# Attention logits: each head on its own 64 rows of the array, without zero-padded queries

## The chip, the cores and the metric

The kernel runs on one core of one Trainium2 chip. The metric is device time in microseconds (us) of one execution. Three runs of the kernel before took 1189.86, 1189.64 and 1187.67 us; the median is 1189.64.

## What is computed

A trunk of four layers on a sequence of 256 tokens of width 1024, all in fp32. Layers 0 and 3 are stick-breaking attention, layer 1 a short convolution, layer 2 gated linear attention; each is followed by a squared-ReLU MLP. Only the attention layers are changed. They have 16 heads of 64 dimensions:

```
z = jnp.einsum('bhqd,bhkd->bhqk', qb, k) * scale
mask = key_pos[None, :] < q_pos[:, None]
log_beta = jax.nn.log_sigmoid(z)
log_1m_beta = jnp.where(mask, jax.nn.log_sigmoid(-z), 0.0)
suffix = lax.cumsum(log_1m_beta, axis=3, reverse=True) - log_1m_beta
weights = jnp.where(mask, jnp.exp(log_beta + suffix), 0.0)
return jnp.einsum('bhqk,bhkd->bhqd', weights, v)
```

## The kernel before

Precision first, since it sets the count of matmuls. TensorE's one-pass fp32 type (fp32r) rounds its operands, so every operand that matters is split into a high part (rounded by ACT) and a low part (the rest, by DVE), and a product is three matmuls: high x high, high x low, low x high. Plain fp32 operands are taken as well; each such product appears as two passes in the trace. All matmuls go through the helper `mm` (line 113), so they share one line and are told apart by tile names: `acc` and `wk` are PSUM tiles (1024 columns in two banks, 512 in one), `hi` and `lo` split weights, `xt` the split input, `cr` and `onesr` constants, `s` anything in the pool of 20 slots of SBUF.

Weights come in by DMA (`raw`, line 207), ACT makes `hi` (line 220) and DVE makes `lo` (line 230). A list fixed in advance gives their order, and a counter how far ahead of use they are made ready.

An attention layer (`sb`, line 558) first makes v for all heads (in layer 0 this belongs to a hand-ordered opening, line 957), then goes over 4 groups of 4 heads, that is of 2 pairs. Two heads of 64 dimensions share the 128 partitions of a q or k tile.

- `qk_steps` (line 575) makes a group's q and k with the weights as the loaded operand: 48 products of 256 columns for each, then the splits. q's is done in two ACT and two DVE instructions of 64 rows each (lines 584 and 586), because each head's queries go to a place of their own: `qpad` has, for each pair of heads, 2 x 256 columns in which head 0 fills rows 0 to 63 of the first 256 and head 1 rows 64 to 127 of the second, and the rest is zero. `padded` (line 552) zeroes four such tiles per layer, on POOL in layer 0 and on DVE in layer 3. k's split is one instruction on each engine (lines 256 and 257).
- `logits` (line 596) handles a pair of heads at a time. Keys are loaded on all 128 rows, and a padded query column meets only its own head's rows. Keys 0 to 127 against all queries of both heads give 512 columns (one bank of the tile `z`), keys 128 to 255 against the later half of the queries 256 columns of the second bank. Two products with the identity put the causal mask (-1e30) in first. Then ACT and DVE make softplus(z) from Abs, Exp and Ln (lines 610 to 615), split in high and low (lines 617 and 618).
- `suffix` (line 621) adds the cumulative sums onto z by products with a triangular matrix of -1 and with a matrix of -1 (`onesr`): per part (high, low) three products of 256, 512 and 256 columns. ACT then takes Exp (line 632).
- `mixed` (line 636) multiplies the weights with v in plain fp32. A head's 64 output dimensions are 64 columns of the array, so these products use the left or the right half of the columns (`128*64` in the trace); they go into the last 256 columns of the second bank, one head on partitions 0 to 63, the other on 64 to 127.

PE's order in the loop over groups (from line 652) is the written one: for each group `logits`, then a stretch of the next group's q and k products (or of the output projection, in the last group) that covers the ACT and DVE chain, then `suffix`, another stretch, and `mixed` for both pairs. `FG` and `FO` (line 67) say how long the stretches are; a step of them is counted at 0.65 us, so 7.15 means 11 steps of six products. The other engines' order is that of a scheduler with priorities.

Of the kernel before, what the change touches and what calls it, by code (L numbers as in the profile page):

```python
# [20 lines left out]
SEQ = 256  # L21
# [41 lines left out]
def hybrid_kernel(ctx: ExitStack, tc: tile.TileContext, x, norm_gains, sb_w_qkv, sb_w_o,  # L63
# [5 lines left out]
    nc = tc.nc  # L69
# [24 lines left out]
    def T(pl, shape, dt, tag):  # L94
        return pl.tile(shape, dt, tag=tag, name=nm(tag))
# [16 lines left out]
    def mm(o, l, r, start, stop):  # L112
        nc.tensor.matmul(out=o, lhsT=l, rhs=r, start=start, stop=stop, skip_group_check=True)  # L113
# [4 lines left out]
    h = []  # L118
# [34 lines left out]
    for kind, l in phases:  # L153
# [14 lines left out]
        elif kind == "sb":  # L168
            w = sb_w_qkv[l // 3]
# [5 lines left out]
        elif kind == "conv":  # L175
            w = conv_w_in[0]
# [5 lines left out]
        else:  # L182
            w = gla_w_in[0]
# [71 lines left out]
    def split(hi, lo, src):  # L255
        nc.scalar.copy(out=hi, in_=src)  # L256
        nc.vector.tensor_tensor(out=lo, in0=src, in1=hi.bitcast(F32), op=ALU.subtract)  # L257
# [187 lines left out]
    def u_pair():  # L445
        return slot((P, 4, SEQ), F32R), slot((P, 4, SEQ), F32R)
# [102 lines left out]
            finish(parts[t] if final and t == NT - 1 else [accs[t]], t)  # L549


    def padded(eng, qpad):
        for i in range(4):
            q = slot((P, 2, 2, SEQ), F32R)
            eng.memset(q.bitcast(F32), 0.0)
            qpad.append(q)

    def sb(l, finish):
        qpad = early[0] if l == 0 else []
        vs = []  # L560
        if l == 0:
            accs = early[1]
        for t in range(NT):
            acc = accs[t] if l == 0 else x_proj(t, (l, "v"))
            v = slot()
            if t == 0:
                nc.vector.tensor_copy(out=v, in_=acc)
            else:
                nc.scalar.copy(out=v, in_=acc)
            vs.append(v)  # L570
            if l and t == 0:
                padded(nc.vector, qpad)
        us = [u_pair(), u_pair()]

        def qk_steps(g, res):
            w = wk_tile()
            yield from w_stat_steps(w, (l, "q", g))

            qh, ql = qpad[2 * (g % 2):2 * (g % 2) + 2]
            wv = w.rearrange("p (a b) -> p a b", b=SEQ)  # L580
            rows_of = [slice(0, 64), slice(64, 128)]
            with tc.high_priority(offset=EP):
                for hd, rs in enumerate(rows_of):
                    nc.scalar.activation(out=qh[rs, :, hd, :], in_=wv[rs, :, :], func=AF.Copy, scale=0.125)
                for hd, rs in enumerate(rows_of):
                    nc.vector.scalar_tensor_tensor(out=ql[rs, :, hd, :], in0=wv[rs, :, :], scalar=0.125,
                                                   in1=qh[rs, :, hd, :].bitcast(F32), op0=ALU.mult, op1=ALU.subtract)
            qs = [(qh[:, j, :, :], ql[:, j, :, :]) for j in range(2)]
            w = wk_tile()
            yield from w_stat_steps(w, (l, "k", g))  # L590
            k = slot((P, 2, 512), F32R)
            with tc.high_priority(offset=EP):
                split(k[:, 0, :], k[:, 1, :], w)
            res[g] = (qs, k)

        def logits(pairs):
            res = []
            for q, k in pairs:
                z = acc_tile()
                z0, z1 = z[:, 0:512], z[:, 512:768]  # L600
                z0v = z0.rearrange("p (a b) -> p a b", b=SEQ)
                mm(z0v[:, :, 0:P], ident_r, msk_r.rearrange("p (a b) -> p a b", b=P), True, False)
                mm(z1, ident_r, msk_r, True, False)
                for a, b in ((0, 0), (0, 1), (1, 0)):
                    mm(z0, k[:, a, 0:P], q[b].rearrange("p a b -> p (a b)"), False, False)
                for a, b in ((0, 0), (0, 1), (1, 0)):
                    mm(z1, k[:, a, P:2 * P], q[b][:, :, P:2 * P], False, False)
                res.append((z, scratch()[:, 0:768], scratch()[:, 0:768], slot((P, 768), F32R), slot((P, 768), F32R)))
            for z, a, sp, sh, sl in res:
                nc.scalar.activation(out=a, in_=z[:, 0:768], func=AF.Abs)  # L610
            for z, a, sp, sh, sl in res:
                nc.scalar.activation(out=a, in_=a, func=AF.Exp, scale=-1.0)
            for z, a, sp, sh, sl in res:
                nc.scalar.activation(out=a, in_=a, func=AF.Ln, bias=1.0)
                nc.vector.scalar_tensor_tensor(out=sp, in0=z[:, 0:768], scalar=0.0, in1=a, op0=ALU.max, op1=ALU.add)
            for z, a, sp, sh, sl in res:
                nc.scalar.copy(out=sh, in_=sp)
                nc.vector.tensor_tensor(out=sl, in0=sp, in1=sh.bitcast(F32), op=ALU.subtract)
            return [(z, sh, sl) for z, a, sp, sh, sl in res]

        def suffix(zs):
            wts = []
            for z, sh, sl in zs:
                z0, z1 = z[:, 0:512], z[:, 512:768]
                z0v = z0.rearrange("p (a b) -> p a b", b=SEQ)
                for n, s in enumerate((sh, sl)):
                    s1 = s[:, 512:768]
                    mm(z1, tri_r, s1, False, n == 1)
                    mm(z0, tri_r, s[:, 0:512], False, False)
                    mm(z0v[:, :, P:2 * P], ones_r, s1.rearrange("p (a b) -> p a b", b=P), False, n == 1)  # L630
                wt = scratch()[:, 0:768]
                nc.scalar.activation(out=wt, in_=z[:, 0:768], func=AF.Exp)
                wts.append((z, wt))
            return wts

        def mixed(pr, zw):
            z, wt = zw
            o = z[:, 768:1024]
            for hd in range(2):
                rows_ = slice(64 * hd, 64 * hd + 64)  # L640
                vc = slice(pr * P + 64 * hd, pr * P + 64 * hd + 64)
                mm(o[rows_, 0:SEQ], vs[0][:, vc], wt[:, hd * SEQ:(hd + 1) * SEQ], True, False)
                mm(o[rows_, P:SEQ], vs[1][:, vc], wt[:, 512 + hd * P:512 + (hd + 1) * P], False, True)
            split(us[pr // 4][0][:, pr % 4, :], us[pr // 4][1][:, pr % 4, :], o)

        rest_of_constants()
        qkv = {}
        Fill(qk_steps(0, qkv))()
        proj = out_proj_steps(l, us, finish)


        with tc.manual_schedule(engines={mybir.EngineType.PE}):
            for g in range(4):
                qs, k = qkv[g]
                fill = Fill(qk_steps(g + 1, qkv)) if g < 3 else Fill(proj)
                if l == 0:
                    ahead[0] = RAMP[g + 1]
                lead, before, after = FG[min(g, 1)] if g < 3 else FO
                fill(lead)
                with tc.high_priority(offset=AP):  # L660
                    zs = logits([(qs[0], k[:, :, 0:SEQ]), (qs[1], k[:, :, SEQ:512])])
# [285 lines left out]
    k, l = phases[0]  # L947
# [9 lines left out]
    def opening():  # L957
# [2 lines left out]

        g8 = slot((P, P))[0:KT, :]
        nc.scalar.dma_start(out=g8, in_=norm_gains[l, pre.get(k, 0), :].rearrange("(k p) -> k p", p=P))
        qpad = []
        padded(nc.gpsimd, qpad)
        still = slot((P, 512), F32R)
        jk = slot()
        accs = [acc_tile() for _ in range(NT)]
# [64 lines left out]
        with tc.manual_schedule(engines={mybir.EngineType.DVE, mybir.EngineType.Activation, mybir.EngineType.PE,  # L1032
# [63 lines left out]
        return qpad, accs  # L1096

    early = opening()
    outv = out.rearrange("b (t p) d -> (b t) p d", p=P)
# [42 lines left out]
```

## Time and profile before

| | us |
|---|---|
| median of three runs | 1189.64 |
| lowest and highest | 1187.67, 1189.86 |
| the profiled execution | 1188.06 |
| its span, from the first to the last instruction | 1186.3 |
| TensorE busy with matmuls (PE) | 1172.3 |
| TensorE busy with weight loads (PEld) | 1009.1 |
| VectorE (DVE) | 802.6 |
| ScalarE (ACT) | 675.1 |
| GpSimd (POOL) | 41.7 |

The mean granted TensorE clock is 0.999 of full speed. A row of the timeline has the start, the time to the end of the last instruction merged into the row, the engine, the line, the operation, the tiles (out<-in), for matmuls the rows x columns of the array that are used (128*128), the shape, and the count. Ends of matmuls are modelled and overlap the next matmul, so the pace is read from starts. Every matmul has a weight load of its own, on the row PEld.

### The profile page before, as it was taken

The numbers are of one execution on the slowest core, as the hardware profiler recorded it, in microseconds if no ns is written. First come the engines' busy times: TensorE is split into PE (matmuls) and PEld (weight loads), VectorE is DVE, ScalarE is ACT, GpSimd is POOL, SyncE is SP. The second block draws the span as 40 slices with busy tenths as digits, with TensorE's granted clock in tenths as the row PEclk, the third lists the DMA queues.
The fourth block names the chain that finished last, engine by engine and source line by source line (L and its number), as shares of the span: only waits on it lengthen the run. The fifth ranks groups of instructions, "written<-read, shape, count | busy, mean of one in ns | idle before, by whom it ended". The sixth has DMA issues, their size and how long they took to land.

```text
span 1186.3 us, 17257 instructions
## 1 busy us (share of the span) xinstructions
PE 1172.3 (99%) x6455; PEld 1009.1 (85%) x6455; DVE 802.6 (68%) x1280; ACT 675.1 (57%) x1212; POOL 41.7 (4%) x80
## 2 busy tenths in 40 slices
PE   8999999999999999999999999999999999999997
PEld 6998888888888888888889888888888998888886
DVE  6865876654878785765776778666658756855651
ACT  5886665543665564554573756545545875654540
POOL 1000100000100100000100010000000001000000
PEclk9999999999999999999999999999999999999999
DMA  7843576666576476666572356666647443666640
GB/s 243 280 125 107 165 244 190 186 196 193 161 234 207 144 236 194 192 193 216 151 242 87 111 161 223 193 197 184 212 145 230 138 157 111 217 195 192 191 146 36
DMA packets 126184, 214.24 MB, mean 181 GB/s; under 512 B 10954, under 2 KB 89042, under 8 KB 126100
## 3 DMA queue, kind: packets, MB, share of 16 engines
q1 hardware_dynamic: 125620, 212.54, 57.8%
q8 instruction: 50, 0.82, 0.3%
q10 hardware_dynamic: 448, 0.59, 0.1%
q14 instruction: 34, 0.28, 0.1%
q0 software_dynamic: 32, 0.00, 0.0%
HBM read 212.07 MB, written 1.05 MB: 180 GB/s over the span
## 4 chain that ended last, share of the span: by engine, by line
PE 93%; DVE 2%; issue 2%; ACT 1%; DMA 1%; POOL 0%; DVEq 0%; POOLq 0%; ACTq 0%
PE acc L113 69%; PE wk L113 22%; PE wk L297 2%; DVE lo L230 1%; DMA raw<-in_gla_w_in_dram 0%; DMA raw<-in_sb_w_qkv_dram 0%; ACT hi L220 0%; DVE lo L227 0%; ACT xt L999 0%; POOL sm L266 0%; DVE s L257 0%; ACT s L271 0%; ACT s L893 0%; DVE s L899 0%; ACT hi L222 0%
## 5 line engine op out<-in xcount | busy, mean ns | idle before, releaser
L230 DVE TENSOR_TENSOR lo<-raw,hi 128x512 fp32r<-128x512 f32 x752 | 492.1, 686 | 212.3 <-ACT hi L220 209.3
L220 ACT CAST hi<-raw 128x512 fp32r<-128x512 f32 x752 | 439.6, 620 | 317.8 <-PE acc L113 170.5
L113 PE MATMUL acc<-hi,s 128*128 128x512 f32 x1216 | 339.5, 391 | 0.0
L113 PEld LDWEIGHTS acc<-hi,s 128*128 128x128 f32 x1216 | 225.6, 188 | 45.8 <-ACT s L256 0.3
L113 PE MATMUL wk<-xt,hi 128*128 128x256 f32 (+1 forms) x1120 | 248.6, 309 | 0.0
L113 PE MATMUL wk<-xt,lo 128*128 128x256 f32 x704 | 196.9, 280 | 0.0
L113 PEld LDWEIGHTS wk<-xt,hi 128*128 128x128 f32 x1120 | 181.4, 188 | 12.8
L113 PE MATMUL acc<-lo,s 128*128 128x512 f32 x608 | 190.4, 390 | 0.0
L113 PE MATMUL acc<-xt,hi 128*128 128x512 f32 x512 | 179.6, 393 | 0.0
L113 PE MATMUL acc<-hi,xt 128*128 128x512 f32 x576 | 160.1, 394 | 0.8 <-ACT hi L220 0.8
L113 PE MATMUL acc<-xt,lo 128*128 128x256 f32 x512 | 143.2, 280 | 0.0
L113 PEld LDWEIGHTS acc<-lo,s 128*128 128x128 f32 x608 | 114.1, 188 | 23.8
L113 PEld LDWEIGHTS wk<-xt,lo 128*128 128x128 f32 x704 | 132.3, 188 | 0.0
L113 PEld LDWEIGHTS acc<-hi,xt 128*128 128x128 f32 x576 | 106.2, 188 | 24.5 <-ACT hi L220 2.3
L113 PEld LDWEIGHTS acc<-xt,hi 128*128 128x128 f32 x512 | 96.1, 188 | 21.0
L113 PEld LDWEIGHTS acc<-xt,lo 128*128 128x128 f32 x512 | 96.3, 188 | 0.9
L113 PE MATMUL acc<-lo,xt 128*128 128x512 f32 x288 | 88.9, 392 | 0.0
L113 PEld LDWEIGHTS acc<-lo,xt 128*128 128x128 f32 x288 | 53.8, 188 | 11.5 <-DVE lo L230 0.3
L284 DVE TENSOR_TENSOR s<-acc,s 128x1024 f32<-128x1024 f32 (+1 forms) x16 | 19.1, 1191 | 59.3 <-ACT s L271 59.0
L263 POOL TENSOR_SCALAR sm<-sm 128x1 f32<-128x1 f32 (+1 forms) x31 | 13.1, 423 | 1052.2 <-ACT s L271 992.8
L113 PE MATMUL acc<-s,s 128*128 128x256 f32 (+3 forms) x314 | 48.3, 330 | 1.0 <-DVE s L257 0.8
L271 ACT ACTIVATE s<-acc 128x1024 f32<-128x1024 f32 (+1 forms) x16 | 16.0, 998 | 57.1 <-PE acc L113 57.1
(125 smaller groups left out, 874.1 us busy)
## 6 DMA issues: line engine op xcount, KB each, us to landing
raw<-in_ffn_w_up_dram SPq DMA_DIRECT2D x128, 512.0 KB, 4.0
raw<-in_ffn_w_down_dram SPq DMA_DIRECT2D x128, 512.0 KB, 3.6
raw<-in_sb_w_qkv_dram SPq DMA_DIRECT2D x48, 512.0 KB, 5.1
raw<-in_conv_w_in_dram SPq DMA_DIRECT2D x24, 512.0 KB, 4.7
raw<-in_gla_w_in_dram SPq DMA_DIRECT2D x24, 512.0 KB, 3.8
raw<-in_sb_w_o_dram SPq DMA_DIRECT2D x16, 512.0 KB, 3.9
s<-in_norm_gains_dram SPq DMA_DIRECT2D x15, 512.0 KB, 5.2
raw<-in_conv_w_out_dram SPq DMA_DIRECT2D x8, 512.0 KB, 4.2
```

Of the source, the lines that this page charges most:

```text
L113: nc.tensor.matmul(out=o, lhsT=l, rhs=r, start=start, stop=stop, skip_group_check=True)
L220: nc.scalar.copy(out=hi[:, cs], in_=raw[:, cs])
L230: nc.vector.tensor_tensor(out=lo[:, cs], in0=raw[:, cs], in1=hi[:, cs].bitcast(F32), op=ALU.subtract)
L263: nc.gpsimd.tensor_scalar(out=v, in0=ss, scalar1=EPS, scalar2=None, op0=ALU.add)
L271: nc.scalar.activation(out=scratch()[:, 0:src.shape[1]], in_=src, func=AF.Square, scale=1.0 / 32.0, accum_out=ss)
L284: nc.vector.tensor_tensor(out=ag[:, cs], in0=a, in1=g[:, cs], op=ALU.mult)
L297: nc.tensor.transpose(out=dst[:, j * P:(j + 1) * P], in_=src[:, j * P:(j + 1) * P], identity=ident)
```

## The change

- `padded` and its calls go, and with them the zero-padded queries. q is split like k, by one ACT and one DVE instruction of 128 x 512, into a tile of its own for each group.
- `logits` now takes both pairs of a group. It puts in the masks of both pairs, then the q-k products. Each product uses one head's 64 rows of q and k (64*128): rows 0 to 63 for head 0, rows 64 to 127 for head 1, in turn. Each head has its own bank of z, in this order of columns: keys 128 to 255 with the later queries (128 columns), keys 0 to 127 with all queries (256), and the v product's output (128).
- `suffix` has per part two products of 384 columns with the triangular matrix, one per head, and two of 128 columns with the matrix of -1.
- `mixed` has three products of 128 columns per head, the two heads in turn; each half of the queries has its output in a bank.
- The tiles of the softplus chain have the shape 2 x 384 instead of 768, with the same number of elements.

The order of PE in the loop over groups, its stretches and the rest of the kernel stay as they are.

```diff
-    def padded(eng, qpad):
-        for i in range(4):
-            q = slot((P, 2, 2, SEQ), F32R)
-            eng.memset(q.bitcast(F32), 0.0)
-            qpad.append(q)
...
-            if l and t == 0:
-                padded(nc.vector, qpad)
...
+            q = slot((P, 2, 512), F32R)
             with tc.high_priority(offset=EP):
-                for hd, rs in enumerate(rows_of):
-                    nc.scalar.activation(out=qh[rs, :, hd, :], in_=wv[rs, :, :], func=AF.Copy, scale=0.125)
-                for hd, rs in enumerate(rows_of):
-                    nc.vector.scalar_tensor_tensor(out=ql[rs, :, hd, :], in0=wv[rs, :, :], scalar=0.125,
-                                                   in1=qh[rs, :, hd, :].bitcast(F32), op0=ALU.mult, op1=ALU.subtract)
-            qs = [(qh[:, j, :, :], ql[:, j, :, :]) for j in range(2)]
+                nc.scalar.activation(out=q[:, 0, :], in_=w, func=AF.Copy, scale=0.125)
+                nc.vector.scalar_tensor_tensor(out=q[:, 1, :], in0=w, scalar=0.125, in1=q[:, 0, :].bitcast(F32),
+                                               op0=ALU.mult, op1=ALU.subtract)
...
-            for q, k in pairs:
-                z = acc_tile()
-                z0, z1 = z[:, 0:512], z[:, 512:768]
-                z0v = z0.rearrange("p (a b) -> p a b", b=SEQ)
-                mm(z0v[:, :, 0:P], ident_r, msk_r.rearrange("p (a b) -> p a b", b=P), True, False)
-                mm(z1, ident_r, msk_r, True, False)
-                for a, b in ((0, 0), (0, 1), (1, 0)):
-                    mm(z0, k[:, a, 0:P], q[b].rearrange("p a b -> p (a b)"), False, False)
-                for a, b in ((0, 0), (0, 1), (1, 0)):
-                    mm(z1, k[:, a, P:2 * P], q[b][:, :, P:2 * P], False, False)
...
+            for j in range(2):
+                z = acc_tile().rearrange("p (h c) -> p h c", h=2)
+                for hd in range(2):
+                    mm(z[:, hd, 0:2 * P], ident_r, msk_r, True, False)
+                res.append((z, logit_tile(F32), logit_tile(F32), logit_tile(F32R), logit_tile(F32R)))
+            for j, (z, *_) in enumerate(res):
+                for ks, out in ((0, z[:, :, P:3 * P]), (P, z[:, :, 0:P])):
+                    for a, b in ((0, 0), (0, 1), (1, 0)):
+                        for hd in range(2):
+                            rs = slice(64 * hd, 64 * hd + 64)
+                            mm(out[:, hd, :], k[rs, a, j * SEQ + ks:j * SEQ + ks + P], q[rs, b, j * SEQ + ks:(j + 1) * SEQ],
+                               False, False)
...
                 for n, s in enumerate((sh, sl)):
-                    s1 = s[:, 512:768]
-                    mm(z1, tri_r, s1, False, n == 1)
-                    mm(z0, tri_r, s[:, 0:512], False, False)
-                    mm(z0v[:, :, P:2 * P], ones_r, s1.rearrange("p (a b) -> p a b", b=P), False, n == 1)
...
+                    for hd in range(2):
+                        mm(z[:, hd, 0:3 * P], tri_r, s[:, hd, :], False, False)
+                    for hd in range(2):
+                        mm(z[:, hd, 2 * P:3 * P], ones_r, s[:, hd, 0:P], False, n == 1)
...
-                mm(o[rows_, 0:SEQ], vs[0][:, vc], wt[:, hd * SEQ:(hd + 1) * SEQ], True, False)
-                mm(o[rows_, P:SEQ], vs[1][:, vc], wt[:, 512 + hd * P:512 + (hd + 1) * P], False, True)
...
+            for first, vt, ws, last_ in ((0, 0, 1, True), (1, 0, 2, False), (1, 1, 0, True)):
+                for hd in range(2):
+                    rs = slice(64 * hd, 64 * hd + 64)
+                    vc = slice(pr * P + 64 * hd, pr * P + 64 * hd + 64)
+                    mm(z[rs, first, 3 * P:4 * P], vs[vt][:, vc], wt[:, hd, ws * P:(ws + 1) * P], vt == 0, last_)
...
-        qpad = []
-        padded(nc.gpsimd, qpad)
```

More of the change, by code (lines that the diff above doesn't have):

```diff
@@ L549, in ffn @@
             finish(parts[t] if final and t == NT - 1 else [accs[t]], t)
-    def padded(eng, qpad):
-        for i in range(4):
-            q = slot((P, 2, 2, SEQ), F32R)
-            eng.memset(q.bitcast(F32), 0.0)
-            qpad.append(q)
     def sb(l, finish):
-        qpad = early[0] if l == 0 else []
         vs = []
         if l == 0:
-            accs = early[1]
+            accs = early
         for t in range(NT):
@@ L577, in qk_steps @@
             yield from w_stat_steps(w, (l, "q", g))
-            qh, ql = qpad[2 * (g % 2):2 * (g % 2) + 2]
-            wv = w.rearrange("p (a b) -> p a b", b=SEQ)
-            rows_of = [slice(0, 64), slice(64, 128)]
+            q = slot((P, 2, 512), F32R)
             with tc.high_priority(offset=EP):
-                for hd, rs in enumerate(rows_of):
-                    nc.scalar.activation(out=qh[rs, :, hd, :], in_=wv[rs, :, :], func=AF.Copy, scale=0.125)
-                for hd, rs in enumerate(rows_of):
-                    nc.vector.scalar_tensor_tensor(out=ql[rs, :, hd, :], in0=wv[rs, :, :], scalar=0.125,
-                                                   in1=qh[rs, :, hd, :].bitcast(F32), op0=ALU.mult, op1=ALU.subtract)
-            qs = [(qh[:, j, :, :], ql[:, j, :, :]) for j in range(2)]
+                nc.scalar.activation(out=q[:, 0, :], in_=w, func=AF.Copy, scale=0.125)
+                nc.vector.scalar_tensor_tensor(out=q[:, 1, :], in0=w, scalar=0.125, in1=q[:, 0, :].bitcast(F32),
+                                               op0=ALU.mult, op1=ALU.subtract)
             w = wk_tile()
@@ L593, in qk_steps, with logit_tile, logits @@
                 split(k[:, 0, :], k[:, 1, :], w)
-            res[g] = (qs, k)
-        def logits(pairs):
+            res[g] = (q, k)
+        def logit_tile(dt):
+            return slot((P, 2, 3 * P), dt)
+        def logits(q, k):
             res = []
-            for q, k in pairs:
-                z = acc_tile()
-                z0, z1 = z[:, 0:512], z[:, 512:768]
-                z0v = z0.rearrange("p (a b) -> p a b", b=SEQ)
-                mm(z0v[:, :, 0:P], ident_r, msk_r.rearrange("p (a b) -> p a b", b=P), True, False)
-                mm(z1, ident_r, msk_r, True, False)
-                for a, b in ((0, 0), (0, 1), (1, 0)):
-                    mm(z0, k[:, a, 0:P], q[b].rearrange("p a b -> p (a b)"), False, False)
-                for a, b in ((0, 0), (0, 1), (1, 0)):
-                    mm(z1, k[:, a, P:2 * P], q[b][:, :, P:2 * P], False, False)
-                res.append((z, scratch()[:, 0:768], scratch()[:, 0:768], slot((P, 768), F32R), slot((P, 768), F32R)))
+            for j in range(2):
[10 more added lines that the diff above has]
+                               False, False)
             for z, a, sp, sh, sl in res:
-                nc.scalar.activation(out=a, in_=z[:, 0:768], func=AF.Abs)
+                nc.scalar.activation(out=a, in_=z[:, :, 0:3 * P], func=AF.Abs)
             for z, a, sp, sh, sl in res:
@@ L614, in logits @@
                 nc.scalar.activation(out=a, in_=a, func=AF.Ln, bias=1.0)
-                nc.vector.scalar_tensor_tensor(out=sp, in0=z[:, 0:768], scalar=0.0, in1=a, op0=ALU.max, op1=ALU.add)
+                nc.vector.scalar_tensor_tensor(out=sp, in0=z[:, :, 0:3 * P], scalar=0.0, in1=a, op0=ALU.max, op1=ALU.add)
             for z, a, sp, sh, sl in res:
@@ L623, in suffix @@
             for z, sh, sl in zs:
-                z0, z1 = z[:, 0:512], z[:, 512:768]
-                z0v = z0.rearrange("p (a b) -> p a b", b=SEQ)
                 for n, s in enumerate((sh, sl)):
-                    s1 = s[:, 512:768]
-                    mm(z1, tri_r, s1, False, n == 1)
-                    mm(z0, tri_r, s[:, 0:512], False, False)
-                    mm(z0v[:, :, P:2 * P], ones_r, s1.rearrange("p (a b) -> p a b", b=P), False, n == 1)
-                wt = scratch()[:, 0:768]
-                nc.scalar.activation(out=wt, in_=z[:, 0:768], func=AF.Exp)
+                    for hd in range(2):
+                        mm(z[:, hd, 0:3 * P], tri_r, s[:, hd, :], False, False)
+                    for hd in range(2):
+                        mm(z[:, hd, 2 * P:3 * P], ones_r, s[:, hd, 0:P], False, n == 1)
+                wt = logit_tile(F32)
+                nc.scalar.activation(out=wt, in_=z[:, :, 0:3 * P], func=AF.Exp)
                 wts.append((z, wt))
@@ L637, in mixed @@
             z, wt = zw
[L638 to L641, printed above, removed]
-                mm(o[rows_, 0:SEQ], vs[0][:, vc], wt[:, hd * SEQ:(hd + 1) * SEQ], True, False)
-                mm(o[rows_, P:SEQ], vs[1][:, vc], wt[:, 512 + hd * P:512 + (hd + 1) * P], False, True)
-            split(us[pr // 4][0][:, pr % 4, :], us[pr // 4][1][:, pr % 4, :], o)
+            for first, vt, ws, last_ in ((0, 0, 1, True), (1, 0, 2, False), (1, 1, 0, True)):
[3 more added lines that the diff above has]
+                    mm(z[rs, first, 3 * P:4 * P], vs[vt][:, vc], wt[:, hd, ws * P:(ws + 1) * P], vt == 0, last_)
+            split(*(us[pr // 4][i][:, pr % 4, :].rearrange("p (h c) -> p h c", h=2) for i in range(2)),
+                  z[:, :, 3 * P:4 * P])
         rest_of_constants()
@@ L653, in sb @@
             for g in range(4):
-                qs, k = qkv[g]
+                q, k = qkv[g]
                 fill = Fill(qk_steps(g + 1, qkv)) if g < 3 else Fill(proj)
@@ L660, in sb @@
                 with tc.high_priority(offset=AP):
-                    zs = logits([(qs[0], k[:, :, 0:SEQ]), (qs[1], k[:, :, SEQ:512])])
+                    zs = logits(q, k)
                 fill(before)
@@ L1095, in opening @@
                         products(which, t, j)
-        return qpad, accs
+        return accs
     early = opening()
```

## The prediction

> **What bounds the kernel now.** I read the page first, then the chain of waits, then the attention layers in windows, then one head group instruction by instruction.
>
> ```profile
> span 1186.3 us, 17257 instructions
> PE 1172.3 (99%) x6455; PEld 1009.1 (85%) x6455; DVE 802.6 (68%) x1280; ACT 675.1 (57%) x1212; POOL 41.7 (4%) x80
> PE 93%; DVE 2%; issue 2%; ACT 1%; DMA 1%; POOL 0%; DVEq 0%; POOLq 0%; ACTq 0%
> ```
>
> TensorE is the chain. The windows of three head groups of the last layer say the same of the place that is changed (us, then PE, PEld, DVE, ACT, POOL busy, clock, DMA share):
>
> ```profile
> 922.90:938.90 16.00, 16.00 (x130) 15.05 (x130) 11.46 (x17) 13.97 (x24) 0.00 (x0) 1.00 0.37 127
> 938.90:956.40 17.50, 17.50 (x143) 16.55 (x142) 11.28 (x17) 14.39 (x24) 0.00 (x0) 1.00 0.36 121
> ```
>
> PE has no free time there, DVE and ACT have 2 to 6 us per group, and the clock is full. So this change is worth what it does to the time that PE needs, plus one stall in layer 0 (below). PE's own rows, from the suffix sums of one group to the logits of the next:
>
> ```profile
> 947.21 0.52 PE L113 MATMUL acc<-s,cr 128*128 128x256 f32 x2
> 947.57 0.28 PE L113 MATMUL acc<-s,onesr 128*128 128x256 f32 x1
> 947.69 0.52 PE L113 MATMUL acc<-s,cr 128*128 128x256 f32 x2
> ...
> 951.58 0.40 PE L113 MATMUL wk<-xt,hi 128*128 128x256 f32 x2
> 951.82 0.28 PE L113 MATMUL wk<-xt,lo 128*128 128x256 f32 x1
> 952.03 1.57 PE L113 MATMUL acc<-s,s 128*64 128x256 f32 x16
> 953.53 0.50 PE L113 MATMUL acc<-cr 128*128 128x256 f32 x2
> 953.87 1.21 PE L113 MATMUL acc<-s,s 128*128 128x512 f32 x6
> 954.92 0.40 PE L113 MATMUL acc<-cr 128*128 128x256 f32 x2
> 955.16 1.22 PE L113 MATMUL acc<-s,s 128*128 128x512 f32 x6
> 956.21 0.40 PE L113 MATMUL wk<-xt,hi 128*128 128x256 f32 x2
> ```
>
> Only starts count here, since matmuls overlap their own tails. A 256-column product takes 0.12 us (951.58 to 951.82 is two of them). The six q-k products of a pair of heads take 953.87 to 954.92, 1.05 us: three of 256 columns at 0.12, so three of 512 at 0.23. One suffix step (products of 256, 512 and 256 columns) takes 0.48. The two mask products take 0.24 (954.92 to 955.16), but 0.34 (953.53 to 953.87) right after the v products, which use 64 columns of the array.
>
> **Term 1, the q-k products.** There are 2 layers x 4 groups x 2 = 16 pairs of heads. Before: 1.05 us each. After: six steps, each a product for head 0 on rows 0 to 63 and one for head 1 on rows 64 to 127; three steps of 256 columns, three of 128. The columns streamed are the same in sum (2,304 per pair); the gain exists only if the two halves run side by side. No row shows products on half the rows. The nearest are the v products on half the columns:
>
> ```profile
> 124.52 0.87 PE wk L297 x8
> ```
> ```profile
> 953.27 0.33 PE L113 MATMUL acc<-s,s 128*64 128x128 f32 x2
> ```
> ```profile
> L113 PE MATMUL acc<-s,s 128*64 128x128 f32 x64 | 6.7, 273 | 0.0
> ```
>
> These eight 128-column fp32 transposes take 0.11 each, so an fp32 pass over 256 columns takes about 0.21. The 16 v passes (eight of 256, eight of 128) would need 8 x 0.21 + 8 x 0.11 = 2.6 us one after the other; they take 1.50 (952.03 to 953.53), so the column halves do run side by side. I take it that row halves do too. Then a step costs what the slower of streaming and weight loading costs. The load of 128 columns has a price:
>
> ```profile
> 643.93 1.89 PE L113 MATMUL wk<-s 128*128 128x64 f32 x16
> 645.63 0.48 PE L113 MATMUL acc<-hi,xt 128*128 128x512 f32 x1
> ```
> ```profile
> L113 PEld LDWEIGHTS acc<-s,cr 128*128 128x128 f32 x64 | 9.9, 188 | 1.3
> L113 PEld LDWEIGHTS acc<-s,s 128*64 128x64 f32 x128 | 9.2, 136 | 2.9 <-issue 0.7
> ```
>
> Sixteen products that move 64 columns against 128 loaded ones take 1.70/16 = 0.11 each, as long as the transposes with twice the columns: the load is the floor. The load records agree: 188 - 136 = 52 ns for 64 columns, so about 0.10 for 128. So after: 3 x 0.12 + 3 x 0.11 = 0.69, a gain of 0.36 per pair, **-5.8 us** over 16. Bounds: if the load were no floor on half the rows, 3 x 0.12 + 3 x 0.06 = 0.54, -8.2 us; if the two loads of a step took turns, 3 x 0.24 + 3 x 0.22 = 1.38, +5.3 us. I take the middle one, because its two assumptions (halves side by side, load as floor) each have a row.
>
> **Term 2, going into and out of half the array.** Into the v products: 951.82 to 952.03 is 0.21 where 0.12 was due, 0.09 lost. Out of them: the last one starts at 953.27 + 0.33 - 0.27 (the duration of one, 273 ns in the lines) = 953.33, and the masks at 953.53, 0.20 later where 0.11 was due: 0.09 lost; then the masks' extra 0.34 - 0.24 = 0.10, which is a weight load that nothing covers. The change adds one such visit per group (masks, then all 24 half-row products, then the projection again): 0.09 + 0.10 in, 0.09 + 0.10 out, 0.38, **+3.0 us** over 8 groups. Bounds: 0 if half-row products need no emptying of the array, 4 if its start is ragged as well.
>
> **Term 3, suffix sums.** A step goes from 256 + 512 + 256 columns (0.48) to 384 + 384 + 128 + 128. A 384-column product lies between 0.12 and 0.23: 0.18. The two of 128 columns stand at the load floor, 0.11. After: 0.58, +0.10, and 16 pairs x 2 steps: **+3.2 us**. Bounds: 0 if floors vanish; above, if a 128-column fp32r product, of which the trace has none, ran at the fp32 price of two 0.11 passes, the step would be 0.80 (a rival below).
>
> **Term 4, the stall in layer 0.** In the first group PE waits for the low half of k:
>
> ```profile
> 42.23 1.39 DVE L586 SCALAR_TENSOR_TENSOR s<-wk,s 64x512 fp32r<-64x512 f32 x2 [0.33 <-ACT s L584]
> 43.65 4.30 DVE L230 TENSOR_TENSOR lo<-raw,hi 128x512 fp32r<-128x512 f32 x7
> ...
> 47.99 0.69 DVE L257 TENSOR_TENSOR s<-wk,s 128x512 fp32r<-128x512 f32 x1
> 48.73 0.86 PE L113 MATMUL acc<-s,s 128*128 128x512 f32 x4 [0.84 <-DVE s L257]
> ```
>
> DVE runs without a break from 42.23 to 48.7. The q split over 128 rows becomes one DVE instruction in place of two (L586, 0.69 each; the like 128x512 instruction, L257, also takes 0.69), so that queue is 0.70 ahead: **-0.7 us**, between 0 (a DMA is then late instead) and -0.84.
>
> **At nothing.** The v products: each column half has three products of two 0.11 passes, 0.66, against 2 x 0.21 + 2 x 0.11 = 0.64; at most 0.05 per pair either way, 0.8 us. The masks: four of 256 columns in both. The memsets of the padded queries:
>
> ```profile
> L555 POOL MEMSET s<- 128x1024 f32 x4 | 3.7, 970 | 0.3 <-POOLq L1126 0.3
> L555 DVE MEMSET s<- 128x1024 f32 x4 | 3.6, 912 | 0.6 <-issue 0.6
> ```
>
> POOL's lie in the first 5 us and POOL's next work waits for DVE; DVE's lie in layer 3, where PE is never late. The cover is PE itself; uncovered they would be worth 3.6 us once. The second ACT instruction of the q split goes too, under the same cover. The ACT and DVE chain from logits to suffix keeps its 768 elements per row. Its last piece:
>
> ```profile
> 945.39 0.95 DVE L618 TENSOR_TENSOR s<-s,s 128x768 fp32r<-128x768 f32 x1
> ```
>
> It ends at 946.34, 0.87 before the suffix at 947.21. The logits block shrinks from 2.68 (953.53 to 956.21) to 0.58 + 0.19 + 1.38 + 0.19 = 2.34, and the first pair ends at 1.46 instead of 1.39, since all four masks go first. That leaves 0.87 - 0.34 - 0.07 = 0.46, so no new wait.
>
> **Sum:** -5.8 + 3.0 + 3.2 - 0.7 = -0.3 us. The profiled execution took 1188.06 us (span 1186.3), the runs' median is 1189.64, 1.6 more; on the median the forecast is **1189.3 us**, no change. About 0.2% (2.4 us) is what a measurement can tell from none.
>
> **Rivals.**
> *Slower: the two halves' loads take turns.* If one load path serves both row halves, a step costs 2 x 0.11 or more, and this decides as soon as the two loads exceed the 0.12 of streaming. Term 1 becomes +5.3, the sum 5.3 + 3.0 + 3.2 - 0.7 = +10.8: 1200.4. For it: nothing in the trace shows two half-row loads at once, and the 64-column loads of the v products are short enough (16 x 0.05 = 0.8 us in 1.5) to fit either way. Against: the same visit overlaps everything else. Products that don't run side by side at all cost the same; that is the change not doing what it says. Chance 0.12.
> *Slower: a load is not hidden behind its own half's product.* Each step is then load plus stream, 0.23 and 0.17; the pair 1.20, +0.15 x 16 = +2.4, sum +7.9: 1197.5. Against it: full-array products of 256 columns keep 0.12 although each has a 0.10 load, so loads run under products of the same rows. Chance 0.06. The Trainium skill, "TensorE: Matmul & The Clock Gate", Part 3 under "What overlaps and what doesn't", has it as a rule: a weight load overlaps matmuls in flight only where the row group differs. By that rule it is 1197.5; the trace's 0.12 speaks against it.
> *Slower: short fp32r products at the fp32 price.* Term 1 -0.5, term 3 (0.80 - 0.48) x 32 = +10.2, sum +12.0: 1201.6. For it: every fp32r product of this kernel moves 256 columns or more, so no row excludes it. Chance 0.07.
> *Faster: no floor or no emptying on half the rows.* With term 1 at -8.2 the sum is -2.7: 1186.9; with term 2 at 0 as well, -5.7: 1183.9. For it: a half-row load fills half the cells. Against: the one load of 8 rows in the lines takes as long as those of 128 (178 against 188 ns):
>
> ```profile
> L1037 PEld LDWEIGHTS wk<-cf,s 8*128 8x128 f32 x1 | 0.2, 178 | 0.6 <-issue 0.6
> ```
>
> Chance 0.25. The Trainium skill, "TensorEngine Tiling (Array Packing)", "Theoretical Speedup", gives up to 2x for a contraction of 64 rows and no load floor; by it term 1 is half of 1.05 x 16, -8.4 us, and the time this rival's.
>
> **How the numbers follow.** Forecast 0.50, with its own range 1186.5 to 1192 (terms 2 and 3 each off by 1.5, the v products by 0.8); slower rivals 0.25; faster 0.25. The range leaves out the rivals at 1200.4 and 1201.6 (0.19) and little else: 1184.0 to 1198.5. Faster by over 0.2%: 0.23 of the fast rival and 0.08 of the forecast's spread, 0.31. Slower: 0.25 + 0.07 = 0.32. Within: 0.37.
>
> **What would show it.** Right: half-row products (64*128) whose two heads start within 0.02 us of each other, steps of 0.12 and 0.11, the 24 of a group in about 1.4 us; a gap of some 0.2 us on each side; suffix steps of 0.58; the layer 0 wait on L257 near 0.1. Wrong: half-row products that start one 0.11 or 0.12 after the other (turns), 128-column fp32r products 0.2 apart, or PE waiting for L618 or L617 ahead of the suffix.

## The result and the profile after

The changed kernel takes 1191.52 us, the median of 11 runs (1191.08 to 1192.98), against 1189.64 for 11 runs of the kernel before (1187.67 to 1192.82). These medians differ by 1.9 us and the means (1191.90 and 1189.31) by 2.6. The ratio of the runs is 1.0021, with an interval from 1.0014 to 1.0029: it is slower by about 2.5 us, about the 2.4 us named as the least that can be told from no change. The forecast was 1189.3. The times go with the mean granted clock: of 27 runs of the kernel before, timed beside a later experiment, 11 at a clock of 0.999 have a median of 1188.33 us and 12 at 0.997 one of 1190.22, and a single run of a later kernel (masks_last), which took 1453.19 us at 0.752, is left out of its ratio.

The page of the profiled execution (1192.27 us) against that of before: the span, the busy times, the chain by engine.

```profile
span 1190.5 us, 17605 instructions
PE 1174.4 (99%) x6647; PEld 1013.9 (85%) x6647; DVE 793.1 (67%) x1268; ACT 671.5 (56%) x1204; POOL 38.8 (3%) x76
PE 92%; DVE 3%; issue 1%; DMA 1%; ACT 1%; POOL 0%; DVEq 0%; POOLq 0%; ACTq 0%
```

DVE, ACT and POOL each do less than before (9.5, 3.6 and 2.9 us less), and yet DVE's share of the chain goes from 2% to 3%. So somewhere PE now waits for a DVE that is less loaded. The span is 4.2 us longer, in three places by the starts of the stages: layer 0 by 1.0, the attention of layer 3 by 1.64 (115.51 to 117.15), and a stretch of the GLA layer, which the change doesn't touch, by 1.56. The last is not the change's doing. PE idles 2.15 us there, for a weight in either kernel, and in some executions its clock then falls for some microseconds. The windows (us, then PE, PEld, DVE, ACT, POOL busy, clock, DMA share, GB/s) of the profiled execution of after, and of a second profile of the same kernel:

```profile
605.00:614.00 9.00, 9.00 (x54) 8.23 (x54) 4.57 (x8) 4.04 (x8) 0.52 (x1) 0.81 0.59 184
```
```profile
605.00:614.00 9.00, 7.69 (x55) 7.26 (x56) 5.85 (x11) 5.61 (x13) 0.52 (x1) 1.00 0.74 254
```

In the second (clock 1.00) the piece takes 91.38 us, as in the kernel before; in the first 92.94. So single profiles of one kernel here differ by 1.5 us in a stage that the change leaves alone, and stages must be compared, not spans. (The 0.81 is a mean over nine us: the clock is 0.51 from 606 to 609 us and 1.00 from 609 on. In the second profile layer 0 was 2.5 longer than before and layer 3 1.6, with a span of 1190.4.)

The place that was changed, by PE's timeline of the changed kernel: the suffix sums, then the turn from one group's v products to the next group's logits.

```profile
950.28 0.57 PE L113 MATMUL acc<-s,cr 128*128 128x384 f32 x2
950.68 0.33 PE L113 MATMUL acc<-s,onesr 128*128 128x128 f32 x2
950.86 0.57 PE L113 MATMUL acc<-s,cr 128*128 128x384 f32 x2
...
954.97 1.53 PE L113 MATMUL acc<-s,s 128*64 128x128 f32 x24
956.43 0.50 PE L113 MATMUL acc<-cr 128*128 128x256 f32 x2
957.29 0.50 PE L113 MATMUL acc<-cr 128*128 128x256 f32 x2 [0.36 <-DVE s L257]
957.72 1.59 PE L113 MATMUL acc<-s,s 64*128 64x256 f32 x24
959.24 0.50 PE L113 MATMUL wk<-xt,hi 128*128 128x256 f32 x2
```

Start to start: a suffix step is 950.86 - 950.28 = 0.58, as forecast. The v products take 956.43 - 954.97 = 1.46, where before they took 1.50. The 24 half-row products take 959.24 - 957.72 = 1.52, half of the way in and out included: the forecast said 1.38 + 0.19 = 1.57. All of this is right. What is new is the row in between: the second pair's masks start 0.86 after the first pair's, where two masks and the way out of the half array took 0.34 before. PE stands for 0.86 - 0.34 = 0.52 us, with "DVE s L257" as the releaser (the 0.36 of the row leaves out the modelled tail of the masks before it). DVE's timeline of that moment says what that is:

```profile
955.61 0.69 DVE L230 TENSOR_TENSOR lo<-raw,hi 128x512 fp32r<-128x512 f32 x1 [3.02 <-ACT hi L220]
956.22 0.68 DVE L257 TENSOR_TENSOR s<-wk,s 128x512 fp32r<-128x512 f32 x1
956.82 0.77 DVE L257 TENSOR_TENSOR s<-acc,s 128x256 fp32r<-128x256 f32 x2
957.50 0.68 DVE L230 TENSOR_TENSOR lo<-raw,hi 128x512 fp32r<-128x512 f32 x1
```

The third row is the low half of the v products' output of both pairs. The first of its two instructions reads the last of the first pair's PSUM tile, and it stands behind k's low half (956.22) and a weight's low part. When it ends, after 0.42 of the row's 0.77, at 957.24, the masks start, at 957.29. There are three of these PSUM tiles, taken in turn; the second pair's z of a group is the tile that the first pair's z of the group before had. Before, the second masks came after the first pair's products, 1.39 us behind the first masks (953.53 to 954.92), and by then the tile was free. DVE's row of the kernel before shows it; the first of its two instructions ended at 954.42:

```profile
954.00 0.74 DVE L257 TENSOR_TENSOR s<-acc,s 128x256 fp32r<-128x256 f32 x2
```

Now the second masks stand ahead of the first pair's products. PE's waits, with total, times and longest: 2.5 us in 7, where before there was one of 0.8, the one in layer 0:

```profile
PE acc L113 <- DVE s L257: 2.5, 7, 0.4
```

One of the seven is the old one (now 0.34); six are new, in groups 1 to 3 (counted from 0) of both layers. The chain of waits of the changed kernel runs through one of them, in layer 0 (start, duration, what): from PE to a weight's split on ACT and DVE, then L257, then PE again.

```profile
61.78 0.63 ACT hi L220
62.41 0.02 issue
62.43 0.69 DVE lo L230
63.12 0.94 DVE s L257 x2
```

### The profile page after: what moved, and what is told of

It reads as the page before. It is cut to its first block, busy times and chain, and to the rows that moved or that the text cites. A ratio compares the mean times of both kernels' runs of the same rounds, so it can differ in the third digit from the quotient of the medians.

```text
span 1190.5 us, 17605 instructions
## 1 busy us (share of the span) xinstructions
PE 1174.4 (99%) x6647; PEld 1013.9 (85%) x6647; DVE 793.1 (67%) x1268; ACT 671.5 (56%) x1204; POOL 38.8 (3%) x76
## 3 DMA queue, kind: packets, MB, share of 16 engines
HBM read 212.07 MB, written 1.05 MB: 179 GB/s over the span
## 4 chain that ended last, share of the span: by engine, by line
PE 92%; DVE 3%; issue 1%; DMA 1%; ACT 1%; POOL 0%; DVEq 0%; POOLq 0%; ACTq 0%
PE acc L113 67%; PE wk L113 23%; PE wk L297 2%; DVE lo L230 1%; DMA raw<-in_sb_w_qkv_dram 1%; DVE s L257 1%; ACT hi L220 1%; DMA raw<-in_gla_w_in_dram 0%; DVE lo L227 0%; ACT xt L986 0%; POOL sm L266 0%; DVE xt L993 0%; ACT s L882 0%; DVE s L888 0%; ACT hi L222 0%
## 5 line engine op out<-in xcount | busy, mean ns | idle before, releaser
L113 PE MATMUL acc<-s,s 128*64 128x128 f32 (+4 forms) x474 | 41.1, 285 | 0.3 <-DVE s L257 0.3
```

## The experiments

**The theory** after the result: half rows gain what was forecast, visits and suffix floor give it back, and on top of that the masks written ahead wait for a PSUM tile, 0.5 to 0.6 us in six groups. **The rival**: that wait is only where PE's time shows; without it PE would stand elsewhere, or the loss lies in the half-row products and their visits, or in layer 0's DMAs. The kernel before was timed beside each, with medians of 1189.3 to 1189.6; each ratio is against it.

**The changed kernel again**, as the measure of the others:

> The changed kernel again, unedited, beside the other two on the same chip. All theories: about 1191.5, 0.2% above the kernel before.

1192.13 us, ratio 1.0021 (1.0012 to 1.0030); the loss repeats. Its L257 waits are the same 2.5 us in 7.

**Free the tile earlier.** ACT copies the v output out of PSUM, and the split reads the copy.

```
-            split(*(us[pr // 4][i]... for i in range(2)), z[:, :, 3 * P:4 * P])
+            o = slot((P, 2, P))
+            nc.scalar.copy(out=o, in_=z[:, :, 3 * P:4 * P])
+            split(*(us[pr // 4][i]... for i in range(2)), o)
```

> Edit: the changed kernel, with PE's order untouched; the v output leaves PSUM in one ACT copy to SBUF, and ACT and DVE make its high and low half from there. The z tile is then free after ACT's 0.38 us and no longer waits for DVE's queue (k's low half, 0.69, and its own low half, 0.42). Theory (PSUM wait): the tile is free about 0.1 us after the last v product, before the second pair's masks want it, so the 0.62 us of 6 groups go: 3.7 us under the changed kernel, about 1187.8. Rival (costs of visits and short products): no change, about 1191.5, or a little above for the added ACT instructions.

1189.23 us, 0.9994 (0.9985 to 1.0003): 2.9 us less than the changed kernel beside it, although ACT has more to do and PE does exactly the same products. The theory had 3.7 less; most of what is missing is a price of the copy (below). PE's timeline at the same turn of the last layer:

```profile
970.58 1.53 PE L113 MATMUL acc<-s,s 128*64 128x128 f32 x24
972.04 0.74 PE L113 MATMUL acc<-cr 128*128 128x256 f32 x4
972.71 1.59 PE L113 MATMUL acc<-s,s 64*128 64x256 f32 x24
974.23 0.74 PE L113 MATMUL acc<-hi,s 128*128 128x512 f32 x2
```

The four masks are one row without a wait, 972.71 - 972.04 = 0.67, where they took 957.72 - 956.43 = 1.29: 0.62 less per group. That is the wait of 0.52 and another 0.10 which the wait had uncovered. DVE's timeline shows that DVE itself was no faster:

```profile
972.50 0.69 DVE L230 TENSOR_TENSOR lo<-raw,hi 128x512 fp32r<-128x512 f32 x1
973.11 0.83 DVE L257 TENSOR_TENSOR s<-s,s 128x256 fp32r<-128x256 f32 x2
```

L257 now ends at 973.94, well after the masks, and nobody waits for it. So it was the tile, and not DVE's pace. The rival (1191.5) falls. The price: behind each layer's last v products the output projection now waits for the split of the copy, and its first product starts 1.78 us after the first of them instead of 1.46. That is 0.6 us over both layers, and PE's waits list it:

```profile
PE acc L113 <- ACT s L256: 0.5, 2, 0.3
```

**One step of the next projection ahead of the logits** in groups 1 and 2, so that PE has work while the tile comes free; group 3 stays as it was. The products are the same; 0.7 us of them move.

```
-FG=((1.3, 7.15, None), (0, 7.8, None))
+FG=((1.3, 7.15, None), (0.65, 7.15, None))
```

> Edit: the changed kernel, with one step of the next group's projection (six products, 0.70 us) moved from the stretch after the logits to the place between the v products and the logits, in groups 1 and 2; group 3 as it was. Theory (PSUM wait): the step covers the 0.62 us, 4 times: 2.5 us under the changed kernel, about 1189.0. Rival (costs of visits and short products): no change from the changed kernel, about 1191.5.

1189.27, 1.0001 (0.9993 to 1.0010). PE's timeline:

```profile
952.67 1.04 PE L113 MATMUL acc<-s,s 128*64 128x128 f32 x16
953.64 0.51 PE L113 MATMUL wk<-xt,hi 128*128 128x256 f32 x2
...
954.46 0.63 PE L113 MATMUL acc<-cr 128*128 128x256 f32 x4
955.02 1.59 PE L113 MATMUL acc<-s,s 64*128 64x256 f32 x24
```

Behind the projection's products the four masks take 955.02 - 954.46 = 0.56, with no wait. In group 3 they still take 1.29, and PE's waits still have three entries, one in layer 0's first group and two in the groups 3:

```profile
PE acc L113 <- DVE s L257: 1.1, 3, 0.4
```

A change of one number in the written order, which takes away four of the six waits, brings back some 2.3 us; the theory had 2.5, and the rival (1191.5) does not allow it.

**Each pair's masks just ahead of its own products**, as in the kernel before; this buys a second visit to half rows per group.

```
             for j in range(2):
                 z = acc_tile().rearrange("p (h c) -> p h c", h=2)
-                for hd in range(2):
-                    mm(z[:, hd, 0:2 * P], ident_r, msk_r, True, False)
...
             for j, (z, *_) in enumerate(res):
+                for hd in range(2):
+                    mm(z[:, hd, 0:2 * P], ident_r, msk_r, True, False)
```

> Edit: the changed kernel, but the second pair's masks are written after the first pair's q-k products instead of ahead of them. Theory (PSUM wait): the second pair's z tile is the previous group's first z tile, which is free only when DVE has made the low half of that group's v output (L257); with all four masks ahead, PE stands 0.62 us for it in 6 of 8 groups. Moving the masks back takes away 6 x 0.62 = 3.7 and adds one more way out of and into half rows, 8 x 0.38 = 3.0: 0.7 us under the changed kernel, about 1190.5, and no PE wait on L257 in groups 1 to 3. Rival (the changed kernel is slower because the half-row visits and the short suffix products cost more than forecast; the wait is only where that shows): 3.0 us above the changed kernel, about 1194.5.

1191.12, 1.0014 (1.0005 to 1.0022), nearer the theory than the rival. PE's timeline:

```profile
955.46 0.50 PE L113 MATMUL acc<-cr 128*128 128x256 f32 x2
955.89 0.91 PE L113 MATMUL acc<-s,s 64*128 64x256 f32 x12
956.73 0.50 PE L113 MATMUL acc<-cr 128*128 128x256 f32 x2
957.16 0.91 PE L113 MATMUL acc<-s,s 64*128 64x256 f32 x12
```

The wait is gone: the second masks come 1.27 after the first. But the visit has a price. From the first masks to the next projection it is now 958.00 - 955.46 = 2.54, against 2.19 with the copy: 0.35 for one visit more, where the prediction had 0.38. (Whole groups, start to start, take 17.77 against 17.42 to 17.50.)

**The masks behind the products**, so that all 24 half-row products come first; the first product into each bank opens the sum.

```
-                for hd in range(2):
-                    mm(z[:, hd, 0:2 * P], ident_r, msk_r, True, False)
...
-                               False, False)
+                               ks == 0 and (a, b) == (0, 0), False)
+            for z, *_ in res:
+                for hd in range(2):
+                    mm(z[:, hd, 0:2 * P], ident_r, msk_r, False, False)
```

> Edit: the changed kernel, with the q-k products of both pairs first (the first product of each bank starts it) and all four masks added after them. Theory (PSUM wait): the first pair's products and the switch into half rows take about 1.0 us, as long as the second z tile needs to come free, so 6 x 0.62 = 3.7 go; and half columns are followed by half rows directly, one switch fewer (0.19) in 6 groups, 1.1: 4.6 to 4.8 us under the changed kernel, about 1187, under the kernel before too. Rival (costs of visits and short products): only the 1.1 goes, about 1190.4.

1189.55, 1.0001 (0.9992 to 1.0011), between the two, and nearer the rival (1190.4) than the theory (about 1187). The timeline, all engines, tells why not less:

```profile
81.28 0.68 DVE L257 TENSOR_TENSOR s<-wk,s 128x512 fp32r<-128x512 f32 x1
...
82.01 1.21 PEld L113 LDWEIGHTS acc<-s,s 64*128 64x128 f32 x20 [0.23 <-DVE s L257]
```

The tile is no longer waited for, but the products start 0.6 earlier and meet k's low half, which ends at 81.96; PE's loads go on at 82.01.

**The products that need k's low half last** as well: in each pair high x high and high x low of both blocks, then low x high of both.

```
-                for ks, out in ((0, z[:, :, P:3 * P]), (P, z[:, :, 0:P])):
-                    for a, b in ((0, 0), (0, 1), (1, 0)):
+                blocks = ((0, z[:, :, P:3 * P]), (P, z[:, :, 0:P]))
+                terms = ((0, 0), (0, 1), (1, 0))
+                for (a, b), (ks, out) in [(t, blk) for two in (terms[:2], terms[2:]) for blk in blocks for t in two]:
```

> Edit: masks_last, and in each pair the two terms with k's high half are done for both blocks of keys before the two with k's low half. Theory: what was left of the wait in masks_last is k's low half (PE stands 0.2 us for L257 of k between the second and third step of the first pair, because the masks no longer give it time); with the low terms last it comes in time, so a group takes 17.33 instead of 17.53 us in groups 1 to 3 and the whole 1.2 us less than masks_last: about 1188.3, just under the kernel before. Rival (PE would stand for the second z tile instead): no difference from masks_last, about 1189.5.

1188.45, 0.9998 (0.9988 to 1.0008). The median is the theory's, but the ratio is only 0.0003 under that of masks_last, and the intervals overlap, so the times alone don't show the gain. In the traces the 24 products of groups 1 to 3 take 1.69 to 1.70 us, where they took 1.81 to 1.82: 0.12 less per group, not 0.2. The timeline shows DVE's two instructions that PE still needs here:

```profile
98.57 0.68 DVE L257 TENSOR_TENSOR s<-wk,s 128x512 fp32r<-128x512 f32 x1
...
99.17 0.77 DVE L257 TENSOR_TENSOR s<-acc,s 128x256 fp32r<-128x256 f32 x2
```

k's low half ends at 99.25 and the product that needs it starts at 99.31; the tile is free at 99.59 (0.42 into the second row) and the second pair starts at 99.64. Either start is about on time. But the step behind each is 0.22 instead of 0.12: what is released at the last moment leaves 0.10 uncovered. What the rival named, the tile as the next wait, is there, only small.

**Both cures together**, the copy and the last order:

> Edit: the same copy, in masks_last_low_last. Theory (what was left there is the second z tile, 0.2 us in 6 groups, behind the same DVE queue): 1.2 us under masks_last_low_last, about 1187.3, 0.15% under the kernel before. Rival (PE's own work is all that is left there): no difference, about 1188.4.

1189.64, 1.0001 (0.9991 to 1.0011). Its profile has the shortest span of all (1185.5), and its two attention layers sum to 239.80 us against 240.64 before. The median shows no gain. At equal clock its runs are lower than those of the kernel before, by 0.6 us at 0.997 (1189.65 against 1190.22) and by 1.0 at 0.999 (1187.28 against 1188.33, from three runs), so a gain of about 0.8 us is likely, but not shown. Against masks_last_low_last the copy takes another 0.1 off the 24 products (1.59) and costs its 0.3 behind each layer's last group, so that the span is shorter by 0.5 (1186.0 to 1185.5), not by the 1.2 of the theory.

**q's split in two again**, the one part of the change that should help layer 0:

```
-                nc.scalar.activation(out=q[:, 0, :], in_=w, func=AF.Copy, scale=0.125)
+                for rs in (slice(0, 64), slice(64, 128)):
+                    nc.scalar.activation(out=q[rs, 0, :], in_=w[rs, :], func=AF.Copy, scale=0.125)
```

and the same for the DVE instruction.

> Edit: the changed kernel, with the q split done in two ACT and two DVE instructions of 64 rows again (unpadded). Theory (the stall of the first group in layer 0 shrank because DVE's queue is one 0.69 us instruction shorter): layer 0's first group starts its next projection 0.7 us later than in the changed kernel, all else the same: 0.7 us above it, about 1192.2. Rival (that stall shrank by 1.5 us because PE has the masks and high products to do meanwhile): no difference, about 1191.5.

1194.73 (five runs), 1.0044 (1.0030 to 1.0058): some 3 us over the changed kernel, more than either theory had. PE's waits:

```profile
PE acc L113 <- DVE s L257: 3.8, 7, 1.0
```

Layer 0's first group waits 1.0 instead of 0.34, the 0.7 of the theory; each of the six other waits is 0.1 longer, which it had left out. That is 1.3 us more in all. The span is 1.5 longer than that of after (1192.0 and 1190.5). Another 0.3 lies outside the span: device time exceeds it by 2.09 to 2.16 us in all five runs, where it is 1.73 to 1.85 in the runs of the other kernels; why stays open. The two profiled executions, both at a mean clock of 0.997, thus differ by 1.8 (1194.09 and 1192.27); the rest of the 3 us is not shown to be the edit's.

**The half rows undone**, all else kept: padded queries on 128 rows, written into the new banks with 256 or 128 columns.

```
-                            mm(out[:, hd, :], k[rs, a, ...], q[rs, b, j * SEQ + ks:(j + 1) * SEQ],
+                            mm(out[:, hd, :], k[:, a, ...], q[b][:, j, hd, ks:SEQ],
```

with `padded` and its split as before.

> Edit: the changed kernel with zero-padded queries again (memsets and split in two as before), every q-k product on all 128 rows, all else as changed (a bank for each head, suffix, v products, masks first). It undoes the half rows alone. Theory (half rows run side by side and their visits cost 0.38 us): 12 full products per pair, 1.38 instead of 0.69 us, no visits: +11.0 - 3.0 + 0.8 for the split in two = 8.8 us above the changed kernel, about 1200.3. Rival (half rows gain little, as the loads are the floor anyway): within 2 us of the changed kernel.

1203.00 (four runs), 1.0117 (1.0103 to 1.0131); the theory had 1200.3. PE's timeline, from the products of one group to the next projection:

```profile
85.98 2.89 PE L113 MATMUL acc<-s,s 128*128 128x256 f32 x24
88.70 0.46 PE L113 MATMUL wk<-xt,hi 128*128 128x256 f32 x2
```

The 24 full products take 2.72 where the half-row ones take 1.52. At the same 24 instructions half rows are thus worth 1.2 us per group, 9.6 over eight. With the waits for L257, 3.4 in place of 2.5, that makes 10.5, the difference of the two spans (1201.0 and 1190.5); the 8.8 of the theory had 8.0 for the products and visits. About 1 us of the 11.5 between the medians stays open. The kernel before had the fewer and wider products of 512 columns, 2 x 1.05 = 2.10. Against that the 24 half-row products are worth 0.58 by themselves, and less with the way in and out (below).

**The two heads not in turn**: within each pair the six products of head 0, then the six of head 1.

```
-                for ks, out in ((0, z[:, :, P:3 * P]), (P, z[:, :, 0:P])):
-                    for a, b in ((0, 0), (0, 1), (1, 0)):
-                        for hd in range(2):
+                for hd in range(2):
+                    for ks, out in ((0, z[:, :, P:3 * P]), (P, z[:, :, 0:P])):
+                        for a, b in ((0, 0), (0, 1), (1, 0)):
```

> Edit: the changed kernel, with the q-k products of a pair written as head 0's six and then head 1's six, instead of in turn. Theory A (each half of the array takes the next instruction of its own, up to several ahead, as the v products of the kernel before did, which were written head by head): no difference from the changed kernel, about 1191.5. Theory B (PE starts products in the written order only, so that in turn is what makes the halves run side by side): six steps of one head and then six of the other, 0.69 us more per pair, 11 us above the changed kernel, about 1202.5.

1194.76 (five runs), 1.0048 (1.0034 to 1.0062), between the theories, neither of which had it. PE's timeline:

```profile
83.46 1.95 PE L113 MATMUL acc<-s,s 64*128 64x256 f32 x24
85.34 0.51 PE L113 MATMUL wk<-xt,hi 128*128 128x256 f32 x2
```

1.88 for the 24, not 1.52, and not the 2.7 of products one after the other. The starts within the row make two series, each some 0.11 apart on average after its first step: one from 83.46, one from 83.81. So the second head, written six products behind the first, begins 0.35 late, beside the first head's third product, and from there the halves run side by side. That the order of starts is not the written one shows in the shapes too: the fourth product to start has 256 columns, while the fourth that is written has 128.

## Why the prediction was right and where it failed

The costs of the products came out nearly as forecast; a wait that the forecast put at nothing made the kernel slower.

**Term 1 and term 2** (-5.8 and +3.0) stand together as what the logits block takes apart from waits. Before it took 2.68 (953.53 to 956.21); with the copy, where nothing waits, 974.23 - 972.04 = 2.19. The way out also reaches into the next row, as the forecast's 0.10 had it: the first two products behind the half rows take 0.34, where they took 0.24 (956.21 to 956.45). So a group has 0.39 less, 3.1 us over eight; the forecast's 2.34 gave 2.8. Both assumptions held. The halves start within 0.02 of each other, and the six steps of a pair take 0.69 (957.94 to 958.63, from the second step of the first pair to that of the second). The starts of the 128-column products are uneven (0.05 to 0.11 apart), but the weight loads are not: the two of a step start within 0.01 of each other, and 0.10 to 0.12 behind those of the step before, for 256 columns and for 128 alike. So the weight load is the floor on half rows too, and 128 columns cost what 256 do. The visit was a little cheaper than forecast, about 0.35.

The turn rival is excluded by the 1.52, and so is the one in which a load is not hidden behind its own half's product: it gave 2 x 1.20 = 2.40 for the 24. The Trainium skill, "TensorE: Matmul & The Clock Gate", Part 3 under "What overlaps and what doesn't", says that a load overlaps running matmuls only where the row group differs, and that matmuls start and end in program order. The runs disagree with the first: 0.12 per step of two products, each of which has a load of about 0.10. With the second, head_by_head's side-by-side halves also disagree: there the second head's series begins beside the first head's third product, ahead of three that are written before it.

**Term 3** (+3.2) came out as said: 0.58 per step, 0.40 for the two products of 384 columns and 0.18 for the two of 128 (forecast 0.36 and 0.22). So short fp32r products do not run at the fp32 price, which would have made the step 0.80; that rival is out. **The v products** were 1.46 for 1.50, inside the 0.05 per pair allowed.

**Term 4** (-0.7): the wait in layer 0 went from 0.84 to 0.34, not to 0.1. The first group there, from its masks to its v products, took 15.93 us before and 15.18 after, 0.75 less; but in the second profile of the changed kernel it took 15.88, because PE waited 0.66 for ACT's high half of k as well. So the term's size stays open between nothing and what was forecast. The prediction also said that PE is never late in layer 3. It was, by 0.2 in that layer's first group (the first pair's six products took 920.19 to 921.45, 1.26 instead of 1.05, behind L257), and the change takes that away too: 14.63 to 14.43.

**The step that failed** is the sentence on the masks under "At nothing", "four of 256 columns in both", and the one that closes that part, "so no new wait". The count is right and the position was seen ("all four masks go first"), but the check that followed was made only for one chain, from the logits to the suffix sums. It did not ask what the moved masks need in order to start: an empty PSUM tile, which a DVE instruction empties that is queued behind k's low half. In place of nothing, the runs show 0.62 us in each of six groups, 3.7 us.

**The sum by the measured terms.** A group that waits takes 18.03 us, start to start, where it took 17.44: 0.59 more. The rows give the same: logits block -0.49, the tile +0.62, the first step behind the half rows +0.10, the suffix sums +0.34 and the step behind them +0.06, the v products -0.04. Over six groups that is +3.5. The two first groups are shorter, by 0.75 (in the first profile) and 0.2. Together that is +2.6, against 2.5 by the ratio. Without the tile's wait it would be about -1.1, where the prediction had -0.3. The two kernels without it (the copy, which has a price of 0.6, and the masks behind) and the one that keeps it in two groups (the step ahead) have ratios of 0.9994 to 1.0001 to the kernel before, with intervals that hold 1. So the forecast of almost no change was about right for the steps that it costed, and the slower result is the step that it passed over.

## What to carry to other kernels

When an instruction is moved ahead in an engine's written order, ask of each operand, and above all of the tile that it writes, who must be done with it and where that one stands in its own queue; an instruction with an unchanged cost can bring a new wait. Products on half the rows pay here against products of 256 columns at the same count (1.2 us per group), but much less against 512-column products (0.4), because each still has its weight load of about 0.11 and each visit costs 0.35. Where PE waits for a tile and not for data, one step of other work in front takes the wait away in each group that has it. An early copy out of PSUM does so too, but here it cost 0.3 us behind each layer's last group, where nothing had waited for the tile.

## What the runs showed of the hardware

- Half-row products overlap even when they are not written in turn, but only with a delay: a head written six products later starts beside the other's third. 1.88 us for 24 products head by head, 1.52 in turn: the written order is worth 0.36 per group, some 3 us.
- A product whose release comes at the last moment starts on time, and the step behind it takes 0.22 instead of 0.12; a wait costs 0.10 more than its length (0.62 for 0.52).
- Going from the full array to 64 rows and back costs about 0.35 us per extra visit. The Trainium skill, "TensorEngine Tiling (Array Packing)", Key Properties, says that a change of tiling mode drains the engine; the runs agree and give the price.
- After 2.15 us of PE idling the granted clock fell to 0.51 (606 to 609 us) and was back at 1.00 from 609 us on in one profile; after the same idle time it stayed at 1.00 in another of the same kernel. The stage took 1.56 us longer in the first.
